# Staged blocks of a conditioned two-layer trunk: the written order is pinned on four engines, and the opening and the first quarter are rewritten

## The chip, the cores and the metric

The kernel runs on one core of a Trainium2 chip. The metric is the device time of one execution in microseconds; lower is better. A core has TensorE (PE, matrix products; PEld is its weight load), VectorE (DVE), ScalarE (ACT), GpSimd (POOL) and SyncE (SP, which here only issues transfers), each with its own instruction queue that is worked off in order, and 16 DMA engines that the queues share.

## The reference

Input x has 256 tokens of 2048 floats, c is one conditioning vector of 2048. There are two layers. In each, `mod = silu(c) @ ada_w[l] + ada_b[l]` gives six vectors of 2048: shift, scale and gate of the mixer, and shift, scale and gate of the feed-forward part (`ada_w[l]` is 2048 x 12288, 100 MB in float32). Then

```
h = rmsnorm(x) * norm_mix_g * (1 + scale) + shift
x = x + gate * mixer(h)          # layer 0: conv module | gated spatial unit; layer 1: pooling
h = rmsnorm(x) * norm_ffn_g * (1 + scale2) + shift2
x = x + gate2 * ((silu(h @ w1) * (h @ w3)) @ w2)
```

and at the end one more rmsnorm. The mixer of layer 0 multiplies h with `ab_w_in` (2048 x 4096); the feed-forward part with `w1` and `w3` (2048 x 5632). All weights are float32 and come from HBM once.

## The kernel before, in words

**Products.** Every weight is brought in as a `raw` tile of 256 rows by 512 columns (512 KB; `load`, L182, issued by SP into a pool of `RAW` = 12 buffers). `split` (L163) makes of it `hi` (a cast on ACT, L167) and `lo` (the remainder, on DVE, L168), four buffers each. A raw buffer is free again when lo is done. A *unit* (L198) is 512 rows by 512 columns, two raw tiles or halves; for each half and each of the two token halves b (128 tokens) there are four matmuls with hi (L216 with the activations' hi, L217 with their lo) and two with lo (L222): 24 matmuls a unit.

**Conditioning.** The scale and shift columns of a quarter (512 of 2048 features) are sums over four steps of two `ada_w` tiles each. `mod_cols` (L368) is a generator: a step loads two tiles and either multiplies them on PE (`ps_ada`, L381) or accumulates on DVE (`accq`, L388), and `put_cols` (L403) turns the sum into columns, by small matmuls into `ps_col`, with `sc`, `gs` or `sh` written by DVE. Scale goes over PE; shift over PE in quarter 0 and over DVE in the others.

**Entries.** For layer 0's mixer and its feed-forward part, `Entry` (L1024) holds the activations. `start` takes the reciprocal root of the mean square (DVE, POOL, L466 to L470); `prep` multiplies a quarter of x by it (`xr`, L477), transposes it on PE (L480) and copies it (`xT`, L518). Once the columns of a quarter are there, `scaled` (L492) applies scale and shift (ACT and DVE), and splits the result into `ah` (ACT) and `al` (DVE).

**Staged blocks.** `started` (L539) begins a projection before the columns of later quarters are known. For each quarter of the input features it scales, and then does three units, which accumulate over the quarters in three pairs of PSUM banks (two pairs `mm`, one pair `mt`). Between the halves of the units it advances the generators of the next quarter's columns (`between`, six slots a quarter). In layer 0's mixer, where nothing is known at the start, 48 MB have to come in for the block; there `params` (L627) runs after quarter 0: it transposes the spatial weights and the convolution's taps, and spreads two norm vectors over the partitions (`to_bcast`, L423), through a single PSUM buffer `ms`. In the feed-forward part of layer 0 the scale columns, and the shift columns up to quarter 1, come from background steps (`tick`, L280) that run with the units of the mixer.

**Order.** The program's text is not the order of the instructions. A scheduler orders them when the program is built, by priority (earlier text first) among those that it takes to be ready by its own estimate of times; each engine's stream is then fixed. A transfer waits in its queue until its buffer is free, and behind the transfers issued before it. The small tables are issued from ACT's queue at the start (L102, L121, L622 to L625), the two halves of x from SP ahead of the first ada tiles.

Of the kernel before, what the change touches and what calls it, by code (L numbers as in the profile page):

```python
# [8 lines left out]
F32 = mybir.dt.float32  # L9
F32R = mybir.dt.float32r  # L10
AF = mybir.ActivationFunctionType
ALU = mybir.AluOpType
PSUM = bass.MemoryType.PSUM

P = 128
# [21 lines left out]
class Trunk:  # L37
# [32 lines left out]
    def consts(self):  # L70
        nc, c = self.nc, self.cpool
        i = self.i
        cs = self.wk.tile([KT, P], F32, name="cs", tag="t", bufs=3)
        nc.sync.dma_start(out=cs, in_=i["c"].rearrange("a (k p) -> (a k) p", p=P))
# [12 lines left out]
        nc.gpsimd.memset(self.pick, 0.0)  # L87
        for j in range(4):
            nc.gpsimd.memset(self.pick[32 * j : 32 * j + 1, :], 1.0)

        ps = self.msp.tile([P, 512], F32, name="ps_c", tag="ms")
# [3 lines left out]
        stage = self.wk.tile([P, P], F32, name="stage", tag="t", bufs=3)  # L95
        nc.vector.memset(stage, 0.0)
# [10 lines left out]
        put("ffn_g", i["norm_ffn_g"].rearrange("l (k p) -> (l k) p", p=P), 2 * KT)  # L107
        put("conv_b", i["a_conv_b"].rearrange("l (k p) -> (l k) p", p=P), HT)
        put("a_g", i["a_norm_g"].rearrange("l (k p) -> (l k) p", p=P), HT)
        put("a_b", i["a_norm_b"].rearrange("l (k p) -> (l k) p", p=P), HT)  # L110
        put("b_bias", i["b_bias"].rearrange("l h t -> (l h) t"), HT)
        ps = self.msp.tile([P, 512], F32, name="ps_c", tag="ms")
        nc.tensor.transpose(ps[:, :P], stage, self.ident)
        cols = c.tile([P, P], F32, name="cols")
        nc.vector.tensor_copy(cols, ps[:, :P])
        self.col = lambda name, k: cols[:, rows[name] + k : rows[name] + k + 1]
        self.cols = lambda name, k, n: cols[:, rows[name] + k : rows[name] + k + n]
        self.adab = c.tile([P, 2, 6 * KT], F32, name="adab")
        for l in range(2):
            st = self.wk.tile([P, P], F32, name="st_b", tag="t", bufs=3)  # L120
            nc.scalar.dma_start(out=st[: 6 * KT, :], in_=i["ada_b"][l].rearrange("(k p) -> k p", p=P))  # L121
            ps = self.msp.tile([P, 512], F32, name="ps_b", tag="ms")
            nc.tensor.transpose(ps[:, : 6 * KT], st[: 6 * KT, :], self.ident[: 6 * KT, : 6 * KT])
            nc.vector.tensor_copy(self.adab[:, l, :], ps[:, : 6 * KT])

# [241 lines left out]

    def mod_cols(self, l, v, q, on_pe, dst, gname=None):  # L368

# [6 lines left out]
        for u in range(4):  # L376
            raws = [self.load(self.i["ada_w"][l], 512 * u + 256 * h, v * D + 512 * q) for h in range(2)]
            for j in range(4):
# [8 lines left out]
                else:  # L387
                    nc.vector.scalar_tensor_tensor(  # L388
                        acc, raws[j // 2][:, j % 2, :], self.cond[:, k : k + 1], acc, op0=ALU.mult, op1=ALU.add
                    )  # L390
            if u < 3:
                yield
# [4 lines left out]
        else:  # L397
            parts = [(acc, self.ones[:, :1])]
        yield
        self.put_cols(parts, 4, l, v, 4 * q, dst, gname)  # L400
# [35 lines left out]
    def norm_cols(self, e, l, sc, sh, gname):  # L436

        e.parts = [
            self.add(self.mod_cols(l, sc, q, True, e.gs, gname), self.mod_cols(l, sh, q, q == 0, e.sh))
            for q in range(4)  # L440
        ]
# [96 lines left out]

    def started(self, e, w_cols, rate, then=None):  # L539

        self.rate = 0.0
        ps = [self.banks(), self.banks()]
        ps.append([self.tpp.tile([P, 512], F32, name=f"mt{b}", tag="tp") for b in range(NB)])
        for g in e.parts[0]:
            self.close(g)
        for q in range(4):
# [56 lines left out]
    def mixer_ab(self, e, nxt):  # L605
        nc, i = self.nc, self.i
        with ExitStack() as s:
# [13 lines left out]
            nc.gpsimd.memset(nrm, 0.0)  # L621
            nc.scalar.dma_start(out=ws, in_=i["b_w_s"][0].rearrange("h t s -> t h s"))  # L622
            nc.scalar.dma_start(out=cwr[:CW, :], in_=i["a_conv_w"][0])
            for n, name in enumerate(("b_norm_g", "b_norm_b")):
                nc.scalar.dma_start(out=nrm[0:64:32, n, :], in_=i[name][0].rearrange("(j n) -> j n", n=512))  # L625

# [18 lines left out]

            for b in range(NB):
                e.start(b)
                for q in range(4):
                    e.prep(b, q)
            held = self.started(e, [(w_in, 0), (w_in, DH), (w_in, 512)], RATES[0], params)  # L650
            act = e.act
# [225 lines left out]
    def ffn(self, p, l, e, nxt, gen_g2, rest):  # L877
# [6 lines left out]
        if e.parts:  # L884
            for q in range(1, 4):
                e.prep(0, q)
            for q in range(4):
                e.prep(1, q)
            ps = self.started(e, [(w1, 0), (w3, 0), (w1, 512)], RATES[1])
            held = {(1, 0): ps[0], (3, 0): ps[1], (1, 1): ps[2]}  # L890
# [76 lines left out]
    def run(self):  # L967
        nc, i = self.nc, self.i
        self.ss = [None] * NB
        self.consts()  # L970
        self.x = []
        for b in range(NB):
            xb = self.xpool.tile([P, D], F32, name=f"x{b}")
            nc.sync.dma_start(out=xb, in_=i["x"][0, b * P : (b + 1) * P, :])
            self.x.append(xb)
            for q in range(4):
                self.sumsq(b, q)

# [9 lines left out]
        self.norm_cols(mix0, 0, SC1, SH1, "mix_g")  # L988
        self.finish(mix0.parts[0][:1])
        self.g1 = self.gate()  # L990
# [86 lines left out]
```

## Time and profile before

| | |
|---|---|
| median of 3 runs | 2014.65 us (2011.18 to 2015.0) |
| profiled execution | 2018.89 us, its span 2017.2 us |
| PE busy, chain of waits on PE | 97%, 95% |
| DVE, ACT, POOL busy | 70%, 42%, 2% |
| moved | 540.39 MB, 268 GB/s over the span |
| granted TensorE clock, mean | 0.982 |

The span is from the first to the last instruction of the profiled execution. A busy PE is one with a matmul in it, which doesn't mean that matmuls follow each other at full speed, so rates are read from the starts of matmuls. The granted clock is 1.0 at full speed and 0.5 after stretches with little work. A row of the timeline has start, duration, engine, line, operation, tiles and count, and in brackets the idle time before it and what ended it.

### The profile page before, as it was taken

To read this page: it belongs to the slowest core of one execution; us is meant where nothing else is said; L and a number is where in the kernel's file an instruction comes from. 1 tells how busy PE (TensorE), PEld (TensorE's weight loads), DVE (VectorE), ACT (ScalarE), POOL (GpSimd) and SP (SyncE) were. 2 spreads that over 40 slices of the span, in tenths; PEclk is the share of its full clock that TensorE was granted. 3 is DMA by queue.
4 is the path that set the end of the run, shared out by engine and by line. 5 is a ranking of instruction groups with operands and counts; after the bars stand their busy time and mean duration, and the time that the engine had idled before them with its cause. 6 is when DMAs were issued, how large, how long until landed. Compare 5 with 4: busy or idle time off the path is not lost.

```text
span 2017.2 us, 24298 instructions
## 1 busy us (share of the span) xinstructions
PE 1957.5 (97%) x8896; PEld 1542.4 (76%) x8896; DVE 1420.8 (70%) x1709; ACT 840.2 (42%) x1023; POOL 34.2 (2%) x91
## 2 busy tenths in 40 slices
PE   5989999998999999999999999999999999999998
PEld 2567677777887888887878887788788888888886
DVE  2667999788778888777887788867555444554455
ACT  3234343454444334443344347544433444334443
POOL 0000000000000000000120000000000000000000
PEclk9889999989999999999999999999999999999999
DMA  9998988879888899888988887889656666566651
GB/s 329 351 369 266 339 277 284 270 252 343 294 277 327 316 341 331 300 295 316 343 308 292 289 286 264 324 276 326 198 187 191 189 189 191 183 189 190 193 184 48
DMA packets 250344, 540.39 MB, mean 268 GB/s; under 512 B 16521, under 2 KB 17849, under 8 KB 249840
## 3 DMA queue, kind: packets, MB, share of 16 engines
q1 hardware_dynamic: 248472, 536.99, 78.2%
q10 hardware_dynamic: 1752, 1.86, 0.3%
q8 instruction: 69, 1.13, 0.2%
q14 instruction: 51, 0.42, 0.1%
HBM read 536.68 MB, written 2.10 MB: 267 GB/s over the span
## 4 chain that ended last, share of the span: by engine, by line
PE 95%; DVE 2%; DMA 2%; ACT 1%; issue 0%; POOL 0%; ACTq 0%; POOLq 0%; DVEq 0%
PE mm L216 28%; PE mm L217 27%; PE mm L222 27%; PE ps_ada L381 3%; PE ps_col L408 2%; PE mt L216 1%; PE mt L217 1%; PE tp L591 1%; PE mt L222 1%; DVE accq L388 1%; PE ps_ada L315 1%; PE tp L480 1%; DMA st_b<-in_ada_b_dram 1%; PE tp L838 1%; DMA raw<-in_pool_w_dram 0%
## 5 line engine op out<-in xcount | busy, mean ns | idle before, releaser
L167 ACT CAST hi<-raw 128x1024 fp32r<-128x1024 f32 x632 | 665.1, 1053 | 986.1 <-PE mm L217 898.2
L168 DVE TENSOR_TENSOR lo<-raw,hi 128x1024 fp32r<-128x1024 f32 x632 | 771.1, 1223 | 423.6 <-ACT hi L167 413.3
L216 PE MATMUL mm<-hi,ah 128*128 128x512 f32 x1568 | 619.5, 396 | 6.0 <-ACT hi L167 3.4
L217 PE MATMUL mm<-hi,al 128*128 128x512 f32 x1568 | 613.6, 392 | 0.0
L222 PE MATMUL mm<-lo,ah 128*128 128x512 f32 x1568 | 422.9, 390 | 0.0
L216 PEld LDWEIGHTS mm<-hi,ah 128*128 128x128 f32 x1568 | 296.0, 189 | 94.3 <-ACT hi L167 14.4
L217 PEld LDWEIGHTS mm<-hi,al 128*128 128x128 f32 x1568 | 296.1, 189 | 62.9 <-DVE accq L388 1.7
L222 PEld LDWEIGHTS mm<-lo,ah 128*128 128x128 f32 x1568 | 295.6, 189 | 61.7
L216 PE MATMUL mm<-hi,hh 128*128 128x512 f32 x704 | 279.9, 398 | 0.0
L217 PE MATMUL mm<-hi,hl 128*128 128x512 f32 x704 | 277.4, 394 | 0.0
L353 DVE SCALAR_TENSOR_TENSOR acc<-raw,cond,acc 128x1024 f32<-128x1024 f32 x180 | 230.6, 1281 | 5.3 <-DMA raw<-in_ada_w_dram 3.7
L222 PE MATMUL mm<-lo,hh 128*128 128x512 f32 x704 | 194.7, 395 | 0.0
L216 PEld LDWEIGHTS mm<-hi,hh 128*128 128x128 f32 x704 | 132.1, 188 | 34.7 <-ACT hi L167 1.7
L222 PEld LDWEIGHTS mm<-lo,hh 128*128 128x128 f32 x704 | 132.1, 188 | 32.1
L217 PEld LDWEIGHTS mm<-hi,hl 128*128 128x128 f32 x704 | 132.1, 188 | 30.8
L388 DVE SCALAR_TENSOR_TENSOR accq<-raw,cond,accq 128x512 f32<-128x512 f32 x135 | 101.1, 749 | 4.8 <-DMA raw<-in_ada_w_dram 2.1
L676 DVE SCALAR_TENSOR_TENSOR co<-aT,cw,co 128x256 f32<-128x256 f32 x240 | 99.5, 479 | 0.0
L216 PE MATMUL mm<-hi,mh 128*128 128x512 f32 x160 | 64.8, 406 | 1.6 <-ACT mh L489 1.6
L599 DVE TENSOR_TENSOR gy<-mm,gate 128x512 f32<-128x512 f32 x72 | 47.1, 686 | 24.3 <-PE mm L222 23.9
L217 PE MATMUL mm<-hi,ml 128*128 128x512 f32 x160 | 63.8, 401 | 0.3 <-DVE ml L490 0.3
L381 PE MATMUL ps_ada<-raw,cond 128*32 128x512 f32 x352 | 62.3, 629 | 0.0
L600 DVE TENSOR_TENSOR x<-x,gy 128x512 f32<-128x512 f32 x72 | 47.2, 688 | 0.1
(169 smaller groups left out, 990.6 us busy)
## 6 DMA issues: line engine op xcount, KB each, us to landing
raw<-in_ffn_w_dram SPq DMA_DIRECT2D x528, 512.0 KB, 4.8
raw<-in_ada_w_dram SPq DMA_DIRECT2D x384, 512.0 KB, 5.7
raw<-in_ab_w_in_dram SPq DMA_DIRECT2D x64, 512.0 KB, 6.5
raw<-in_ab_w_out_dram SPq DMA_DIRECT2D x32, 512.0 KB, 5.7
raw<-in_pool_w_dram SPq DMA_DIRECT2D x8, 512.0 KB
x<-in_x_dram SPq DMA_DIRECT2D x2, 1024.0 KB, 6.5
gate<-in_final_g_dram SPq DMA_DIRECT2D x1, 1024.0 KB
out_dram<-x SPq DMA_DIRECT2D x2, 512.0 KB
```

The source lines that it names most:

```text
L167: nc.scalar.copy(hi, raw)
L168: nc.vector.tensor_tensor(lo, raw, hi.bitcast(F32), op=ALU.subtract)
L216: nc.tensor.matmul(ps[b], act[b][0][:, kk, :], hi[:, k, :], start=first and kk == 0, stop=False)
L217: nc.tensor.matmul(ps[b], act[b][1][:, kk, :], hi[:, k, :], start=False, stop=False)
L222: self.nc.tensor.matmul(ps[b], act[b][0][:, kk, :], lo[:, k, :], start=False, stop=last and kk == 3)
L353: nc.vector.scalar_tensor_tensor(acc, raw, self.cond[:, k : k + 1], acc, op0=ALU.mult, op1=ALU.add)
L381: nc.tensor.matmul(acc[32 * j : 32 * j + 32, :], self.cond[:, k : k + 1].to_broadcast([P, 32]), raws[j // 2][:, j % 2, :], start=u == 0, s ...
L388: nc.vector.scalar_tensor_tensor(acc, raws[j // 2][:, j % 2, :], self.cond[:, k : k + 1], acc, op0=ALU.mult, op1=ALU.add)
L408: nc.tensor.matmul(ps[:, a : a + 1], src[:, P * a : P * a + P], one, start=u == 0, stop=u == len(parts) - 1,)
L599: nc.vector.tensor_tensor(t, ps, g[:, 512 * q : 512 * q + 512], op=ALU.mult)
L600: nc.vector.tensor_tensor(xs, xs, t, op=ALU.add)
L676: nc.vector.scalar_tensor_tensor(co[:, k, :], src, cw[:, k, j : j + 1], co[:, k, :], op0=ALU.mult, op1=ALU.add,)
```

## The change

`in_order` collects what is traced inside it and gives every instruction on PE, DVE, ACT and SP an edge to the one before it in the text on the same engine. The edges make no instruction wait at run time; they only forbid the scheduler another order. Both calls of `started` stand inside it, and in the mixer a new `opening` too, into which the loading of x, the small tables, the columns of quarter 0 and the preparation of both token halves have moved. The small tables are now issued by SP; the spatial weights, taps and norm vectors (`tables`) after quarter 0, and `params` follows quarter 1 rather than quarter 0.

In `started`, quarter 0 cuts the tiles of the first two units at once, and takes tokens 0 through both units before tokens 1; tokens 1 are scaled only then. In the feed-forward part the seven transposes after the first become hooks ahead of the half units. The other units are written out, with a slot for the generators behind each half; the staged columns (quarters 1 to 3 of the mixer) have one yield more after their last load and none before `put_cols`, so that the copy of the sum and `put_cols` stand together in the fifth slot.

```diff
+    @contextmanager
+    def in_order(self):
+        traced = self.nc.cur_bb.bb.instructions
+        n = len(traced)
+        yield
+        before = {}
+        for ins in traced[n:]:
+            if ins.engine in ORDERED:
+                if ins.engine in before:
+                    self.tc.add_manual_dep(ins, before[ins.engine].name, AFTER, reason="in_order")
+                before[ins.engine] = ins
...
+    def opening(self, e):
+        nc, c, i = self.nc, self.cpool, self.i
+        sc, sh = e.parts[0]
...
+        def tokens(b):
+            nc.sync.dma_start(out=self.x[b], in_=i["x"][0, b * P : (b + 1) * P, :])
+            for q in range(4):
+                self.sumsq(b, q)
+
+        def entry(b):
+            e.start(b)
+            for q in range(4):
+                e.prep(b, q)
...
-            nc.scalar.dma_start(out=stage[r : r + n, :], in_=ap)
+            nc.sync.dma_start(out=stage[r : r + n, :], in_=ap)
...
+        next(sc)
+        next(sc)
+        tokens(0)
+        next(sc)
         put("mix_g", i["norm_mix_g"].rearrange("l (k p) -> (l k) p", p=P), 2 * KT)
+        tokens(1)
+        entry(0)
+        next(sc)
         put("ffn_g", i["norm_ffn_g"].rearrange("l (k p) -> (l k) p", p=P), 2 * KT)
...
+        next(sh)
         put("conv_b", ...)
...
+        next(sh)
...
+            nc.tensor.transpose(ps[:, : 6 * KT], st[l][: 6 * KT, :], self.ident[: 6 * KT, : 6 * KT])
+            nc.vector.tensor_copy(self.adab[:, l, :], ps[:, : 6 * KT])
+        entry(1)
         ps = self.msp.tile([P, 512], F32, name="ps_c", tag="ms")
         nc.tensor.transpose(ps[:, :P], stage, self.ident)
...
+        self.close(sc)
+        next(sh)
+        next(sh)
+        self.close(sh)
...
         for q in range(4):
-            e.act[q] = [self.scaled(e.act[q][b], q, b, e.gs, e.sh) for b in range(NB)]
             nxt = e.parts[q + 1] if q < 3 else ()
+            if q == 0:
+                cuts = [cut(w, 0, col0) for w, col0 in w_cols[:2]]
+                for b in range(NB):
+                    e.act[0][b] = self.scaled(e.act[0][b], 0, b, e.gs, e.sh)
+                    for n in range(4):
+                        u, h = divmod(n, 2)
+                        for f in hooks.get((b, n), ()):
+                            f()
+                        self.products(*cuts[u][h], h, e.act[0], b, ps[u], True)
+                        self.products_lo(*cuts[u][h], h, e.act[0], b, ps[u], False)
+                        if h == 1:
+                            self.between(nxt, 2 * b + u)
...
+            else:
+                e.act[q] = [self.scaled(e.act[q][b], q, b, e.gs, e.sh) for b in range(NB)]
             for u, (w, col0) in enumerate(w_cols):
-                self.unit(
-                    w, 512 * q, col0, e.act[q], ps[u], q == 0, q == 3, lambda: self.between(nxt, 2 * u)
-                )
-                self.between(nxt, 2 * u + 1)
-            if q == 0 and then is not None:
-                then()
+                if q == 0 and u < 2:
+                    continue
+                for h, (hi, lo) in enumerate(cut(w, q, col0)):
+                    for b in range(NB):
+                        self.products(hi, lo, h, e.act[q], b, ps[u], q == 0)
+                    for b in range(NB):
+                        self.products_lo(hi, lo, h, e.act[q], b, ps[u], q == 3)
+                    self.between(nxt, 2 * u + h)
+                self.after_unit()
+            if q in then:
+                then[q]()
...
-            held = self.started(e, [(w_in, 0), (w_in, DH), (w_in, 512)], RATES[0], params)
+            with self.in_order():
+                self.opening(e)
+                held = self.started(
+                    e, [(w_in, 0), (w_in, DH), (w_in, 512)], RATES[0], {0: tables, 1: params}
+                )
...
+            late = [(1, 0), (0, 1), (1, 1), (0, 2), (1, 2), (0, 3), (1, 3)]
+            slots = [(0, 1), (0, 2), (0, 3), (1, 0), (1, 1), (1, 2), (1, 3)]
+            hooks = {at: [lambda c=c: e.prep(*c)] for at, c in zip(slots, late)}
+            with self.in_order():
+                ps = self.started(e, [(w1, 0), (w3, 0), (w1, 512)], RATES[1], hooks=hooks)
```

More of the change, by code (lines that the diff above doesn't have):

```diff
@@ L1 @@
-from contextlib import ExitStack
+from contextlib import ExitStack, contextmanager
 import concourse.bass as bass
@@ L13 @@
 PSUM = bass.MemoryType.PSUM
+ENG = mybir.EngineType
+ORDERED = (ENG.PE, ENG.DVE, ENG.Activation, ENG.SP)
+AFTER = mybir.DependencyInfo(mybir.DependencyClass.NoSync, mybir.DependencyReason.DATA)
 P = 128
@@ L101, in put @@
             nonlocal r
-            nc.scalar.dma_start(out=stage[r : r + n, :], in_=ap)
+            nc.sync.dma_start(out=stage[r : r + n, :], in_=ap)
             rows[name] = r
             r += n
+        next(sc)
+        next(sc)
+        tokens(0)
+        next(sc)
         put("mix_g", i["norm_mix_g"].rearrange("l (k p) -> (l k) p", p=P), 2 * KT)
+        tokens(1)
+        entry(0)
+        next(sc)
         put("ffn_g", i["norm_ffn_g"].rearrange("l (k p) -> (l k) p", p=P), 2 * KT)
+        st = [self.wk.tile([P, P], F32, name=f"st_b{l}", tag="t", bufs=3) for l in range(2)]
+        for l in range(2):
+            nc.sync.dma_start(out=st[l][: 6 * KT, :], in_=i["ada_b"][l].rearrange("(k p) -> k p", p=P))
+        next(sh)
         put("conv_b", i["a_conv_b"].rearrange("l (k p) -> (l k) p", p=P), HT)
@@ L111, in consts @@
         put("b_bias", i["b_bias"].rearrange("l h t -> (l h) t"), HT)
+        next(sh)
+        self.adab = c.tile([P, 2, 6 * KT], F32, name="adab")
+        for l in range(2):
+            ps = self.msp.tile([P, 512], F32, name="ps_b", tag="ms")
+            nc.tensor.transpose(ps[:, : 6 * KT], st[l][: 6 * KT, :], self.ident[: 6 * KT, : 6 * KT])
+            nc.vector.tensor_copy(self.adab[:, l, :], ps[:, : 6 * KT])
+        entry(1)
         ps = self.msp.tile([P, 512], F32, name="ps_c", tag="ms")
@@ L117, in consts @@
         self.cols = lambda name, k, n: cols[:, rows[name] + k : rows[name] + k + n]
[L118 to L124, printed above, removed]
+        self.close(sc)
+        next(sh)
+        next(sh)
+        self.close(sh)
     def bands(self, tiles):
@@ L366, in mod_full, with mod_cols @@
             yield
-    def mod_cols(self, l, v, q, on_pe, dst, gname=None):
+    def mod_cols(self, l, v, q, on_pe, dst, gname=None, staged=False):
         nc = self.nc
@@ L390, in mod_cols @@
                     )
-            if u < 3:
+            if u < 3 or staged:
                 yield
@@ L398, in mod_cols @@
             parts = [(acc, self.ones[:, :1])]
-        yield
+        if not staged:
+            yield
         self.put_cols(parts, 4, l, v, 4 * q, dst, gname)
@@ L438, in norm_cols @@
         e.parts = [
-            self.add(self.mod_cols(l, sc, q, True, e.gs, gname), self.mod_cols(l, sh, q, q == 0, e.sh))
+            self.add(
+                self.mod_cols(l, sc, q, True, e.gs, gname, staged=q > 0),
+                self.mod_cols(l, sh, q, q == 0, e.sh, staged=q > 0),
+            )
             for q in range(4)
@@ L543, in started, with cut @@
         self.rate = 0.0
         ps = [self.banks(), self.banks()]
[L545 removed]
         for g in e.parts[0]:
             self.close(g)
+        def cut(w, q, col0):
+            raws = [self.load(w, 512 * q + 256 * h, col0) for h in range(2)]
+            return [self.split(raw) for raw in raws]
         for q in range(4):
[L549 removed]
             nxt = e.parts[q + 1] if q < 3 else ()
[L551 to L557 removed]
+            if q == 0:
[10 more added lines that the diff above has]
+                            self.between(nxt, 2 * b + u)
+                for _ in range(2):
+                    self.after_unit()
+                ps.append([self.tpp.tile([P, 512], F32, name=f"mt{b}", tag="tp") for b in range(NB)])
+            else:
+                e.act[q] = [self.scaled(e.act[q][b], q, b, e.gs, e.sh) for b in range(NB)]
+            for u, (w, col0) in enumerate(w_cols):
+                if q == 0 and u < 2:
[6 more added lines that the diff above has]
+                    self.between(nxt, 2 * u + h)
+                self.after_unit()
+            if q in then:
+                then[q]()
@@ L621, in mixer_ab, with tables @@
             nc.gpsimd.memset(nrm, 0.0)
[L622 to L625, printed above, removed]
+            def tables():
+                nc.sync.dma_start(out=ws, in_=i["b_w_s"][0].rearrange("h t s -> t h s"))
+                nc.sync.dma_start(out=cwr[:CW, :], in_=i["a_conv_w"][0])
+                for n, name in enumerate(("b_norm_g", "b_norm_b")):
+                    nc.sync.dma_start(out=nrm[0:64:32, n, :], in_=i[name][0].rearrange("(j n) -> j n", n=512))
             def params():
@@ L644, in params @@
                 self.to_bcast(nrm[:, 1, :], bb, 2)
[L646 to L649, printed above, removed]
-            held = self.started(e, [(w_in, 0), (w_in, DH), (w_in, 512)], RATES[0], params)
+            with self.in_order():
+                self.opening(e)
+                held = self.started(
+                    e, [(w_in, 0), (w_in, DH), (w_in, 512)], RATES[0], {0: tables, 1: params}
+                )
             act = e.act
@@ L970, in run @@
         self.consts()
[L971 to L977, printed above, removed]
+        self.x = [self.xpool.tile([P, D], F32, name=f"x{b}") for b in range(NB)]
         def cols(name):
```

17 lines of the change are left out of this document (6 added, 11 removed).

## The prediction

> **What bounds the kernel now.** I read the page's totals, slices and chain of waits first, then a table of stretches, then the timeline of the two places that the change rewrites.
>
> ```profile
> span 2017.2 us, 24298 instructions
> PE 1957.5 (97%) x8896; PEld 1542.4 (76%) x8896; DVE 1420.8 (70%) x1709; ACT 840.2 (42%) x1023; POOL 34.2 (2%) x91
> GB/s 329 351 369 266 339 277 284 270 252 343 294 277 327 316 341 331 300 295 316 343 308 292 289 286 264 324 276 326 198 187 191 189 189 191 183 189 190 193 184 48
> PE 95%; DVE 2%; DMA 2%; ACT 1%; issue 0%; POOL 0%; ACTq 0%; POOLq 0%; DVEq 0%
> ```
>
> TensorE carries 95% of the chain, so a microsecond by which a staged block ends earlier or later is a microsecond at the end. The first three slices (some 150 us) move the most bytes. The next rows say why (columns: stretch, length, busy time of PE, PEld, DVE, ACT, POOL with counts, granted clock, DMA share, GB/s).
>
> ```profile
> 2.00:4.00 2.00, 0.26 (x1) 0.18 (x1) 0.00 (x0) 0.81 (x2) 1.02 (x2) 1.00 0.74 197
> 18.00:21.00 3.00, 0.13 (x1) 0.16 (x1) 0.00 (x0) 0.00 (x0) 0.00 (x0) 1.00 0.18 66
> 30.00:84.00 54.00, 44.21 (x209) 26.79 (x208) 28.80 (x47) 18.18 (x29) 0.00 (x0) 0.84 1.05 386
> 72.00:76.00 4.00, 3.65 (x14) 3.21 (x14) 3.02 (x7) 2.86 (x6) 0.00 (x0) 0.50 1.05 388
> ```
>
> From 30 to 84 us DMA is full at 386 GB/s and TensorE isn't: the first staged block is bound by the load stream. A load of 524 KB costs the stream 1.36 us. After a wait the clock is 0.50 (72 to 76), so a matmul then costs twice its time.
>
> ```profile
> 8.09 21.34 SPq L185 DMA_DIRECT2D raw<-in_ada_w_dram  x16
> 45.89 0.80 PE L216 MATMUL mm<-hi,ah 128*128 128x512 f32 x1 [3.39 <-ACT hi L167]
> 82.48 0.50 PE L216 MATMUL mm<-hi,ah 128*128 128x512 f32 x1
> 117.53 0.39 PE L216 MATMUL mm<-hi,ah 128*128 128x512 f32 x1
> 147.66 0.39 PE L216 MATMUL mm<-hi,ah 128*128 128x512 f32 x1
> 158.54 0.39 PE L216 MATMUL mt<-hi,ah 128*128 128x512 f32 x1
> 163.98 0.39 PE L216 MATMUL mm<-hi,ah 128*128 128x512 f32 x1
> ```
>
> These are the first products of quarters 0, 1, 2 and 3 of the first staged block, then the last unit and its end. A unit's 24 matmuls from 158.54 to 163.98 make 0.227 us each: 2.7 us for a half unit, 16.3 us for a quarter of three units. The block ends at 163.98; that is the number to beat.
>
> **The change, part by part.** Four engines now follow the text, so I walk the text with the durations of before. Loads are counted from 1 in SP's new order: 8 for the scale, 8 for the shift (x between them), 4 for the first two units, 16 for quarter 1's columns, 2 for the third unit, then 22 per quarter.
>
> *The opening.* The ada loads no longer wait till 8.09, so the stream flows from about 3 us (half of the stretch 2 to 4 was full) and load 12 lands near 26 us (8.5 MB at 386 GB/s, plus half a microsecond for small transfers queued between). From there the chain is one of small steps.
>
> ```profile
> 12.43 0.42 PE L123 MATMUL ps_b<-ident,st_b 96*128 96x96 f32 x1 [0.38 <-DVE cols L115]
> 12.88 0.26 DVE L124 COPY adab<-ps_b 128x96 f32<-128x96 f32 x1 [0.51 <-PE ps_b L123]
> 21.48 0.15 DVE L466 TENSOR_REDUCE s<-ss 128x1 f32<-128x4 f32 x1
> 22.49 1.28 DVE L477 TENSOR_SCALAR xr<-x,r 128x512 f32<-128x512 f32 x3 [0.68 <-POOL r L470]
> 36.16 4.55 PE L381 MATMUL ps_ada<-raw,cond 128*32 128x512 f32 x32
> 40.81 0.59 ACT L395 COPY rows<-ps_ada 128x512 f32<-128x512 f32 x1 [5.23 <-PE ps_ada L381]
> 41.45 1.05 PE L408 MATMUL ps_col<-pick,rows 128*128 128x1 f32 x8 [0.74 <-ACT rows L395]
> 435.02 3.20 PE L480 MATMUL tp<-ident,xr 128*128 128x128 f32 x12 [0.69 <-ACT xT L518]
> ```
>
> Shift step (a quarter of 4.55) to 27; two bias transposes with copies 1.7, to 28.7; the norm of tokens 1 (21.48 to 22.49) 1.0; xr and four transpose groups at 1.07 (3.20 for three) with the last copy 5, to 34.7; the table of columns 0.8; scale columns 1.1; two shift steps 2.2; rows 0.7; shift columns 1.1: 40.6. ScalarE casts the four waiting halves only behind the rows copy, and VectorE subtracts them before it scales the activations:
>
> ```profile
> L167 ACT CAST hi<-raw 128x1024 fp32r<-128x1024 f32 x632 | 665.1, 1053 | 986.1 <-PE mm L217 898.2
> L168 DVE TENSOR_TENSOR lo<-raw,hi 128x1024 fp32r<-128x1024 f32 x632 | 771.1, 1223 | 423.6 <-ACT hi L167 413.3
> L388 DVE SCALAR_TENSOR_TENSOR accq<-raw,cond,accq 128x512 f32<-128x512 f32 x135 | 101.1, 749 | 4.8 <-DMA raw<-in_ada_w_dram 2.1
> 73.14 0.88 ACT L500 ACTIVATE h<-xT,sh,gs 128x128 f32<-128x128 f32 x2 [4.01 <-DVE sh L414]
> 74.86 0.61 ACT L489 CAST ah<-h 128x512 fp32r<-128x512 f32 x1
> 76.78 0.69 DVE L490 TENSOR_TENSOR al<-h,ah 128x512 fp32r<-128x512 f32 x1
> ```
>
> Four lo at 1.22 from 40.6 end at 45.5, then 0.7 for h and 0.7 for ah: first product at 47.0 against 45.89. **The opening itself gains nothing**; it could lie 2 us to either side.
>
> *Tokens 0 ahead.* Unit 0 for tokens 0 at half clock 5.4 and its scale step 2, to 54.4; three more such pieces at 2.7 + 1.1, to 65.8. Nothing waits on tokens 1. Loads 33 and 34 need the buffers that the scale step at 54.4 frees, so the stream has a gap of some 3 us (0 if the clock is up at once) and load 38 lands near 64.3 (22.2 MB take 57.5, plus 3 and the gap). Third unit's first half 2.7, both column sums 2, scaling both token halves 2 x (0.88 + 0.61) = 3, next hi 1.05: quarter 1's first product at 74.7 against 82.48. **Here the change is 8 us ahead.**
>
> *Tables.* They leave ScalarE's queue at the start, where they shared the loss at 18 to 21, for SP's queue ahead of quarter 1's loads. The 512 KB of b_w_s cost 1.4. The 124 KB of a_conv_w cost 0.3 spread over 16 engines, or 124 KB / (386/16 GB/s) = 5.2 on one. In before its neighbour on that queue took long:
>
> ```profile
> 9.77 10.97 DMA st_b<-in_ada_b_dram
> ```
>
> 48 KB issued just behind it landed after 10.97 us, the end of it while DMA ran at 66 GB/s (18 to 21): a sixth of full, with something unfinished. That is nearest to one engine, so I take 4.9 beside the even share; both ends stay. So quarter 1's last load lands at 64.3 + 1.4 + 4.9 + 22 x 1.36 = 100.5.
>
> [...]
>
> *Params.* Before, its transposes and broadcasts lay between products (73 to 93). Now they stand in the text behind quarter 1, and quarter 2's scaling, splits, accumulations and products stand behind them on ACT, DVE and PE. One PSUM buffer makes them a chain:
>
> ```profile
> 83.28 0.60 PE L636 MATMUL tp<-ident,prm 128*128 128x128 f32 x4
> 83.92 0.69 DVE L637 COPY wcT<-tp 128x512 f32<-128x512 f32 x1 [1.04 <-PE tp L636]
> 84.73 0.43 PE L641 MATMUL tp<-ident,prm 31*128 31x31 f32 x4
> 85.20 0.29 DVE L642 COPY cw<-tp 128x124 f32<-128x124 f32 x1 [0.20 <-PE tp L641]
> 88.42 0.69 DVE L490 TENSOR_TENSOR rlo<-nrm,rhi 128x512 fp32r<-128x512 f32 x1 [0.71 <-PE ps_bc L432]
> 91.71 0.43 PE L432 MATMUL ps_bc<-rhi,identr 128*128 128x512 f32 x1
> 92.41 0.59 ACT L434 COPY bgb<-ps_bc 128x512 f32<-128x512 f32 x1 [0.82 <-PE ps_bc L433]
> ```
>
> Two rounds from 83.28 to 85.6 (2.33 each) are 4.7; four broadcasts at 1.4 (91.71 to 93.1) are 5.6; the two rlo that stand ahead of a pair add 1.4: 11.7. Counted from the last load (100.5): first half and column sums to +4.6, second half to +7.4, params to +19.1, scaling 3 and hi 1.05 to +23.2, that is 123.7; without params +8.9, 109.4. The twelve raw buffers cover 12 x 1.36 = 16.3 us of it, then DMA stands still for some 10. Quarter 2 can't catch up: its first piece runs at half clock (7.4), the next three take 3.8 each, the loads for its last column step can only be issued when the second step frees buffers, and VectorE has 4 lo and 16 accq (16.9) plus the last two lo before the turn. I get 28.9 to quarter 3's first product: 152.6 against 147.66. **The 8 us ahead have become 5 behind.** Plus 16.3: the block ends at 168.9, **+4.9**. If the chain cost nothing, quarter 3 would start at 100.5 + 8.9 + 29.9 = 139.3; that end of the bound is the rival below.
>
> *Second staged block.* Before:
>
> ```profile
> 430.75 0.66 PE L480 MATMUL tp<-ident,xr 128*128 128x128 f32 x4 [1.25 <-DVE xr L477]
> 442.72 0.79 PE L216 MATMUL mm<-hi,ah 128*128 128x512 f32 x1 [0.25 <-ACT ah L489]
> 503.32 2.27 PE mm L216 x4
> ```
>
> The first product can follow the first transpose group directly: 430.75 + 0.66 + copy 0.6 + 0.9 + 0.6 = 434 rather than 442.72. But seven groups (0.66) now lie between products, the first at half clock, so quarter 0 ends near 459.5; before it ended 19 us (16.3 and a cold start) after 442.72, near 462: 2.4 gained. Quarters 1 and 2 are bound by VectorE: 16 accq (12.0), 6 lo (7.3) and scaling (two al at 0.69, four h at some 0.3: 2.6) are 22, and in text order it also idles some 3 at a turn, when only the columns are awaited. 459.5 + 21.4 + 24.7 = 505.6 for the last quarter's first product, against 503.32 followed by 3 us lost to half clock. Together **-0.3**, bounded by -5 (all of the early start stays) and +4 (every accq delays a lo).
>
> Moved memsets and the two yields of the staged columns cost nothing: GpSimd is 2% busy, and the columns are summed behind a half unit of 2.7. If that cover were gone they would cost 2 per turn.
>
> **Sum:** +4.9 - 0.3 = about +5. The profiled execution took 2018.89 (span 2017.2) and would take 2024. The median of the runs, 2014.65, lies 4.2 below it: 2020.
>
> **Rivals.**
> - *It evens out, about 2015.* a_conv_w spreads (-4.9), or the stream has no gap at 55 us (-3). For it: each term is of the size of the sum. Against: the 10.97 us of its neighbour.
> - *Faster, about 2006.* The place is the turn from quarter 1 to quarter 2: if buffers and loads in flight hide the params chain, the stage stays bound by the stream and ends at 139.3 + 16.3 = 155.6, that is -8.4. For it: before, the same work cost little among products. Against: one PSUM buffer and the text order. It decides from the point where quarter 2's first product comes before 119 (123.7 - 4.9).
> - *Slower still, about 2026.* In the second block VectorE's fixed order (3.0 of accq ahead of each 1.22 of lo, against 2.7 of products) holds TensorE in each of eight slots: the +4 end, and the +5 stays, with some 2 more for half clock. For it: VectorE needs 22 per quarter and TensorE 16.3. Against: the slots lend each other time through four split buffers.
>
> **How the numbers follow.** Forecast (+2 to +9) 0.42, evens out 0.22, faster 0.27, slower still 0.09. The likeliest one's own range is 2016 to 2025. The range must reach the faster case's centre with some room, 2003, and the end of the slower one, 2029. What this kernel's runs can tell from no change is about 0.2%, 4 us: the forecast lies just above it. Slower takes most of the forecast and the slower case, 0.47; same 0.24; faster takes its rival and a little of the rest, 0.29.
>
> **What would show it.** Right: first product near 47, quarter 1's near 75, params rows in a stretch of some 12 us with hardly a product of the block in it and DMA well below 386 GB/s for about 10 us after it, quarter 2's first product near 124, end near 169; in the second block a first product near 434 and a last quarter that starts no earlier against the first block's end than before. Wrong: params rows with products between them, a first product before 42, or a first block that ends before 160.

## The result and the profile after

The changed kernel takes 2046.42 us (median of 4 runs, 2044.93 to 2048.26), the kernel before beside it on the same chip 2014.83 us: a ratio of 1.0158, interval 1.0139 to 1.0177. It is slower by 31.6 us, 27 more than forecast and 17 above the range. The profiled execution took 2047.44 us, 28.55 more than that of before.

From the page of the changed kernel (totals, slices, chain of waits):

```profile
span 2045.7 us, 24280 instructions
PE 1966.1 (96%) x8896; PEld 1545.2 (76%) x8896; DVE 1423.4 (70%) x1708; ACT 840.0 (41%) x1023; POOL 35.4 (2%) x92
GB/s 329 364 228 296 337 302 257 267 308 166 329 286 349 331 302 302 304 326 339 307 293 293 341 260 275 299 317 306 226 178 188 193 187 193 184 182 197 189 187 50
PE 87%; DVE 2%; DMA 1%; issue 1%; ACT 1%; POOL 0%; POOLq 0%; DVEq 0%; ACTq 0%
```

The busy times hardly move, but TensorE's share of the chain of waits falls from 95% to 87%, and two slices of the stream drop: the third (102 to 153 us) from 369 to 228 GB/s, the tenth (460 to 511) from 343 to 166. Those are the two staged blocks.

From the timeline of the changed kernel, the first products of quarters 0 to 3 and the first one behind the block, for the first block and then the second:

```profile
48.30 0.80 PE L249 MATMUL mm<-hi,ah 128*128 128x512 f32 x1 [6.03 <-ACT ah L526]
77.44 0.64 PE L249 MATMUL mm<-hi,ah 128*128 128x512 f32 x1 [2.58 <-ACT hi L200]
133.10 0.80 PE L249 MATMUL mm<-hi,ah 128*128 128x512 f32 x1 [4.99 <-ACT hi L200]
161.47 0.50 PE L249 MATMUL mm<-hi,ah 128*128 128x512 f32 x1 [1.82 <-ACT hi L200]
179.59 0.39 PE L249 MATMUL mm<-hi,ah 128*128 128x512 f32 x1
...
457.12 0.80 PE L249 MATMUL mm<-hi,ah 128*128 128x512 f32 x1 [7.47 <-ACT ah L526]
485.18 0.50 PE L249 MATMUL mm<-hi,ah 128*128 128x512 f32 x1 [0.77 <-ACT hi L200]
510.76 0.57 PE L249 MATMUL mm<-hi,ah 128*128 128x512 f32 x1
536.51 0.50 PE L249 MATMUL mm<-hi,ah 128*128 128x512 f32 x1 [0.28 <-ACT hi L200]
553.27 0.39 PE L249 MATMUL mm<-hi,ah 128*128 128x512 f32 x1
```

and the end of the second block in the kernel before:

```profile
522.72 0.39 PE L216 MATMUL mm<-hi,ah 128*128 128x512 f32 x1
```

The first block ends at 179.59 instead of 163.98: **+15.6**. From there to the end of the second block it is 373.7 us instead of 358.7: **+14.9**. Behind it 1494.2 are left instead of 1496.2: -2.0. Together that is the difference of the two profiled executions, 28.55.

**The turn to quarter 2.** The last load of quarter 1 is cast at 104.83; from then to 133.10 it is 28.3 us. Timeline of the changed kernel:

```profile
104.83 1.04 ACT L200 CAST hi<-raw 128x1024 fp32r<-128x1024 f32 x1 [0.30 <-DMA raw<-in_ab_w_in_dram]
112.45 0.63 PE L249 MATMUL mt<-hi,ah 128*128 128x512 f32 x1
112.88 0.63 PE L250 MATMUL mt<-hi,al 128*128 128x512 f32 x1
115.56 0.60 PE L715 MATMUL tp<-ident,prm 128*128 128x128 f32 x4
121.63 0.58 ACT L468 COPY bgb<-ps_bc 128x512 f32<-128x512 f32 x1 [14.76 <-PE ps_bc L467]
128.15 0.58 ACT L468 COPY bgb<-ps_bc 128x512 f32<-128x512 f32 x1 [1.31 <-PE ps_bc L467]
128.63 0.88 ACT L537 ACTIVATE h<-xT,sh,gs 128x128 f32<-128x128 f32 x2
```

Its table of stretches (columns as in the prediction):

```profile
115.00:120.00 5.00, 2.88 (x19) 2.02 (x17) 1.80 (x4) 0.00 (x0) 0.00 (x0) 0.84 0.22 81
120.00:125.00 5.00, 2.83 (x5) 1.37 (x5) 1.08 (x3) 1.69 (x3) 0.00 (x0) 0.50 0.00 2
125.00:130.00 5.00, 2.44 (x4) 0.79 (x3) 0.88 (x3) 2.41 (x5) 0.00 (x0) 0.50 0.00 0
130.00:135.00 5.00, 1.90 (x5) 1.53 (x6) 3.82 (x6) 4.45 (x8) 0.00 (x0) 0.50 0.00 0
```

The rows of params take 13.2 us (115.56 to 128.73). ScalarE waits 14.76 us for the first broadcast with everything of quarter 2 behind it, the transfers stand still for 15 us (the last column is 2, 0, 0), and the clock falls to 0.50.

**Quarter 0 of the second block.** Timeline of the changed kernel, then its table:

```profile
449.00 0.66 PE L517 MATMUL tp<-ident,xr 128*128 128x128 f32 x4 [1.25 <-DVE xr L514]
453.31 1.21 DVE L201 TENSOR_TENSOR lo<-raw,hi 128x1024 fp32r<-128x1024 f32 x1
455.21 26.19 SPq L218 DMA_DIRECT2D raw<-in_ada_w_dram  x4
456.02 0.34 DVE L539 TENSOR_SCALAR h<-xT,gs,sh 128x128 f32<-128x128 f32 x1
456.45 0.62 ACT L526 CAST ah<-h 128x512 fp32r<-128x512 f32 x1 [4.65 <-DVE h L539]
464.45 0.16 DVE L448 TENSOR_TENSOR sh<-ps_col,adab 128x4 f32<-128x4 f32 x1 [6.26 <-PE ps_col L442]
487.43 0.48 DVE L419 TENSOR_SCALAR accq<-raw,cond 128x512 f32<-128x512 f32 x1
```

```profile
457.00:465.00 8.00, 7.30 (x24) 5.69 (x24) 1.66 (x6) 0.65 (x2) 0.00 (x0) 0.60 0.43 162
465.00:481.00 16.00, 13.69 (x70) 10.91 (x71) 5.64 (x12) 7.58 (x13) 0.00 (x0) 1.00 0.01 2
```

For 16 us nothing is loaded (2 GB/s), while VectorE works 5.64 us of 16. SP's four loads from 455.21 take 26.19 us to issue: there is no free buffer. By the order of SP's loads two of the twelve buffers hold quarter 0's third unit and ten what quarter 1 and the next shift columns need. The first `accq` of those columns, which would free some, runs at 487.43, behind all of quarter 0 in the text. In the kernel before the same sum began at 450.91, in the middle of its quarter 0, where the scheduler had put it:

```profile
450.91 0.48 DVE L386 TENSOR_SCALAR accq<-raw,cond 128x512 f32<-128x512 f32 x1
460.00:465.00 5.00, 5.00 (x24) 4.14 (x23) 4.93 (x7) 2.11 (x2) 0.00 (x0) 1.00 1.05 381
```

### The profile page after: what moved, and what is told of

Read it like the earlier page. It is cut to its first block, busy times and chain, and to the rows that moved or that the text cites. A ratio compares the mean times of both kernels' runs of the same rounds, so it can differ in the third digit from the quotient of the medians.

```text
span 2045.7 us, 24280 instructions
## 1 busy us (share of the span) xinstructions
PE 1966.1 (96%) x8896; PEld 1545.2 (76%) x8896; DVE 1423.4 (70%) x1708; ACT 840.0 (41%) x1023; POOL 35.4 (2%) x92
## 3 DMA queue, kind: packets, MB, share of 16 engines
q10 hardware_dynamic: 288, 1.05, 0.1%
## 4 chain that ended last, share of the span: by engine, by line
PE 87%; DVE 2%; DMA 1%; issue 1%; ACT 1%; POOL 0%; POOLq 0%; DVEq 0%; ACTq 0%
PE mm L249 27%; PE mm L250 26%; PE mm L255 26%; PE ps_ada L414 1%; PE tp L668 1%; PE ps_col L442 1%; DMA raw<-in_ffn_w_dram 1%; PE ps_ada L348 1%; DVE accq L421 1%; DVE lo L201 1%; PE mt L255 1%; PE mt L249 1%; PE mt L250 1%; PE tp L917 1%; PE tp L517 0%
## 5 line engine op out<-in xcount | busy, mean ns | idle before, releaser
L421 DVE SCALAR_TENSOR_TENSOR accq<-raw,cond,accq 128x512 f32<-128x512 f32 x135 | 101.2, 750 | 13.8 <-DMA raw<-in_ada_w_dram 10.7
L255 PE MATMUL mm<-lo,mh 128*128 128x512 f32 x160 | 47.3, 405 | 0.0
```

The lines of the kernel that those rows point to most:

```text
L255: self.nc.tensor.matmul(ps[b], act[b][0][:, kk, :], lo[:, k, :], start=False, stop=last and kk == 3)
L421: nc.vector.scalar_tensor_tensor(acc, raws[j // 2][:, j % 2, :], self.cond[:, k : k + 1], acc, op0=ALU.mult, op1=ALU.add)
```

## The experiments

Each group was timed beside the kernel before on one chip; its median there was 2016.2 in the first group, 2016.64, 2017.22 and 2017.08 in the others. Differences are to that median ("over before"); the change itself is 31.6 over before.

**First group: the order or the text?** The written order was made a switch for each block, and in one kernel the instructions traced in `params` were left out of it.

```
-            if ins.engine in ORDERED:
+            if ins.engine in ORDERED and self.pins:
...
-        for ins in traced[n:]:
-            if ins.engine in ORDERED:
+        for k, ins in enumerate(traced[n:], n):
+            if ins.engine in ORDERED and not self.loose[0] <= k < self.loose[1]:
```

No order in either block:

> The changed kernel without any of the order edges: the new text, left to the scheduler. Theory A (the order edges cost the time, because ACT, DVE and SP can't go past what waits): most of the 31.6 us comes back, 2012 to 2024 us, and no stretch of ten us without DMA in either block. Rival B (the new text costs it: the opening, tokens 0 ahead, tables on SP): 2040 or more.

2020.63 us, ratio 1.0022 (1.0011 to 1.0033), 4.4 over before. Block 1 ends at 167.3, and block 2 takes 359.3 us from there.

Order in the mixer block alone, and in the feed-forward block alone:

> Order edges in the mixer's block alone. Theory A: the second block loses nothing against before, so some 12 us less than the changed kernel, about 2034 us; first block ends near 180 us as in the changed kernel. Rival B: about 2046 us, with the second block as slow as in the changed kernel.

> Order edges in the feed-forward block alone. Theory A: the first block ends near 164 us as before instead of 180, so about 2030 us; the second block still takes some 12 us more than before. Rival B: the first block ends near 180 us, about 2046 us.

2032.71 us, ratio 1.0083 (1.0061 to 1.0106): block 1 ends at 178.6, then 360.3 to the end of block 2. And 2030.14 us, ratio 1.0075 (1.0055 to 1.0096): 167.3, then 371.0. Against the run without an order, the order in one block alone costs 12.1 (mixer) and 9.5 us (feed-forward) by the medians. In both it costs 27.2, so 5.6 us more than the sum; what makes them isn't shown. The text without an order costs 4.4.

> Both blocks with their order edges, but the instructions of params left out of the edges, so that the scheduler may put them among the products of quarter 2. Theory A as the prediction put it (the params chain delays quarter 2 by some 14 us and the stream can't make it up): quarter 2 starts near 114 us instead of 133, the first block ends 12 to 16 us earlier, about 2032 us. Rival (the stream is what is late, by a_conv_w on one DMA engine and the late first quarter): the block ends at most 4 us earlier, about 2043 us.

2029.06 us, ratio 1.0070 (1.0050 to 1.0090). With params alone outside the order, block 1 ends at 165.6, 14 us earlier, and block 2 keeps its loss (372.1). That is no later than without any order (167.3): in block 1 the order costs nothing but at this one place.

**Second group: which engine, which load?** Four edits, each in a kernel of its own: VectorE left out of the order in the feed-forward block (`self.free`), a_conv_w in two loads, the order of SP alone, and no order with other places of tables and params (and a_conv_w in two loads there too).

```
-            if ins.engine in ORDERED:
+            if ins.engine in ORDERED and ins.engine not in self.free:
...
-                nc.sync.dma_start(out=cwr[:CW, :], in_=i["a_conv_w"][0])
+                for r0, r1 in ((0, 16), (16, CW)):
+                    nc.sync.dma_start(out=cwr[r0:r1, :], in_=i["a_conv_w"][0, r0:r1])
...
-ORDERED = (ENG.PE, ENG.DVE, ENG.Activation, ENG.SP)
+ORDERED = (ENG.SP,)
...
-RATES[0], {0: tables, 1: params}
+RATES[0], {0: params}, {(0, 0): [tables]}
```

> Everything as in the changed kernel, but in the feed-forward block VectorE's instructions are left out of the written order; the mixer block is pinned on all four engines as before. Theory A (in the second block the cost is VectorE's written order: the sums of the second column step stand behind quarter 0, so twelve buffers fill and the loads stop): the sums run during quarter 0 again, the stretch from 460 to 481 us moves well over 200 GB/s, the block lasts 84 us from its first product as with no written order there instead of 96, and the time is 2034 (2031 to 2038). Rival B (the cost lies in TensorE's or ScalarE's written order, the transpose groups between the products): the loads stop as before and the time stays above 2042.

2032.68 us, ratio 1.0086 (1.0068 to 1.0103); block 2 takes 357.4 us behind block 1. Theory A holds: in the stretch that it named, 460 to 481 us, the loads move 269 GB/s. Table of stretches and timeline of this run:

```profile
465.00:481.00 16.00, 15.77 (x76) 12.80 (x75) 15.67 (x21) 11.22 (x16) 0.00 (x0) 1.00 0.91 295
463.86 7.04 DVE L421 SCALAR_TENSOR_TENSOR accq<-raw,cond,accq 128x512 f32<-128x512 f32 x9
```

Nine `accq` in a row run in the middle of quarter 0; VectorE is busy 15.67 of 16 us instead of 5.64, and the stream moves 295 GB/s instead of 2. TensorE's transposes between the products, still pinned here, cost nothing that shows.

> The load of a_conv_w (31 rows) is issued as two, of 16 and of 15 rows; nothing else changes. Theory A (the 31 rows go over few DMA engines, so the stream runs at 106 to 319 GB/s from 72 to 78 us): this dip goes, the last load of quarter 1 lands 2 to 4 us earlier than 104.8, the first staged block ends as much earlier, and the time is 2043 (2041 to 2045). Rival B (the dip comes from full buffers, VectorE being late with the halves that free them): the dip stays and the time is 2046.

2038.45 us, ratio 1.0123 (1.0099 to 1.0146). The dip goes; first the changed kernel, then this one:

```profile
74.00:76.00 2.00, 0.86 (x4) 0.38 (x2) 1.26 (x4) 1.20 (x3) 0.00 (x0) 1.00 0.30 106
```

```profile
74.00:76.00 2.00, 2.00 (x14) 1.78 (x14) 0.76 (x3) 0.90 (x3) 0.00 (x0) 1.00 1.01 366
101.41 1.05 ACT L200 CAST hi<-raw 128x1024 fp32r<-128x1024 f32 x1 [0.32 <-DMA raw<-in_ab_w_in_dram]
```

The last load of quarter 1 is cast at 101.41 instead of 104.83, 3.4 us earlier, although the first product of this run comes 4.0 later (52.29; last section). The block's end comes 3.5 earlier (176.1), but the same pinned block ends at 178.6 and 177.1 in two other runs (order in the mixer block alone; VectorE free in the feed-forward block), so how much of this is the load's isn't shown. The time fell by more than that, some 8 us, below the expected range; another 3.2 lie between the blocks, in a part that no order holds, and 1.5 in the second block. What moved there isn't settled.

> Both blocks keep the written order of the loads (SP) alone; TensorE, VectorE and ScalarE are left free. Theory A (what costs is that work which is ready has to stand behind work which isn't, on the three computing engines): as with no written order at all, 2021 (2017 to 2025). Rival B (the order of the loads itself delays what is needed first): 2030 or more, with the first staged block's end past 172 us.

2020.07 us, ratio 1.0020 (1.0010 to 1.0031): as with no order at all. The order of the loads alone costs nothing that shows.

> The new text without any written order; the tables are issued behind the first four halves' loads, a_conv_w in two pieces, and the transposes and broadcasts of params stand behind quarter 0 as in the kernel before. Theory A (without the written order the new opening is 4 us ahead at its first product, and what it loses by the end of the first block, 3 us, comes from the tables and params standing later): the first block ends at 163 or before, 2014 (2010 to 2018). Rival B (the loss comes from the order of tokens 0 ahead of tokens 1 and its backlog on TensorE): 2020, with the first block's end near 167.

2013.65 us, ratio 0.9990 (0.9980 to 1.0000), 3.0 below before. Block 1 ends at 159.3. The 4.4 us of the text without an order were the places of tables and params and the 31-row load together, not tokens 0 ahead of tokens 1, which stays here.

**Third group: does it add up, and is it the place or the order?**

> As the run with no written order and early tables, but the feed-forward block has the text of the kernel before (all transposes ahead, the quarters unit by unit). Theory A (without a written order the new text of the second block costs some 4 us by itself: there the block took 84.3 us from its first product to its end, before it took 80.0): what the first block gains, 8.6 us at the second block's first product, reaches the end, and the time is 2010 (2006 to 2013). Rival B (the gain is given back after the second block whatever its text, by transfers that were ahead anyway): 2013 to 2015.

2013.46 us, ratio 0.9988 (0.9978 to 0.9997): no gain from the old text of the second block. It takes 358.8 us behind the first with it and 359.1 with the new text. Theory A falls: that the span from the first product differs (80 to 84 us) only says that this product comes earlier.

> As the changed kernel with its written order, with two things left out of it: the instructions of params in the mixer block, and VectorE in the feed-forward block. Theory A (these two places are the whole cost of the written order, each by work that stands behind something that waits): each gave 17 and 14 us by itself, together 2016 (2013 to 2020). Rival B (the gains overlap, what one gives is lost at the other): 2025 or more.

2019.81 us, ratio 1.0023 (1.0011 to 1.0035), 2.6 over before. With the order kept everywhere but for params in the mixer block and VectorE in the feed-forward block, 29 of the 31.6 us are gone.

> As the run beside it with both places left out of the written order, and a_conv_w loaded in two pieces of 16 and 15 rows. Theory A (the 31 rows cost the stream 2 to 3 us where it bounds the block): 2 to 4 us below the run beside it. Rival B (once the stalls are gone the block is bound elsewhere, or the 8 us that this edit gave in the changed kernel were the clock's phase or another order of the free part): within 1 us of it.

2013.57 us, ratio 0.9990 (0.9979 to 1.0001): 6.2 below its neighbour, more than expected. The last load of quarter 1, first in the neighbour, then in this run:

```profile
106.00 1.05 ACT L200 CAST hi<-raw 128x1024 fp32r<-128x1024 f32 x1 [0.31 <-DMA raw<-in_ab_w_in_dram]
```

```profile
99.55 1.05 ACT L200 CAST hi<-raw 128x1024 fp32r<-128x1024 f32 x1 [0.31 <-DMA raw<-in_ab_w_in_dram]
```

It is cast 6.45 us earlier, but here the first products lie 3.6 apart the other way (52.06 and 48.42), ahead of the edited load. So both pairs mix the load with the opening, with opposite signs. With the 31 rows in one load the cast comes at 103.9 to 104.8 where the first product comes at 48 to 49 (three runs: the changed kernel, and those with the order in the mixer block alone and with VectorE free), and at 105.6 to 106.5 where it comes at 52 (three runs: params outside the order, params last, and the neighbour). In two pieces it comes at 99.55 and 101.41. At the same opening the load costs 4.2 to 5.3 us, and the later opening some 1.8.

> The changed kernel with all its written order, but params stands behind quarter 3 of the mixer block instead of behind quarter 1. Theory A (the chain costs what is queued behind it: at the turn it holds the scaling and the splits that free the buffers, at the end only work outside the written order follows): quarter 2's first product comes near 119, no stretch without transfers, the first block's products end near 166, and the time is 2032 (2028 to 2036). Rival B (the chain costs its 13 us wherever it stands, then with the convolution waiting for its results): 2042 or more.

```
-                    e, [(w_in, 0), (w_in, DH), (w_in, 512)], RATES[0], {0: tables, 1: params}
+                    e, [(w_in, 0), (w_in, DH), (w_in, 512)], RATES[0], {0: tables, 3: params}
```

2033.73 us, ratio 1.0090 (1.0072 to 1.0108). Timeline and table of stretches of this run:

```profile
116.74 0.50 PE L249 MATMUL mm<-hi,ah 128*128 128x512 f32 x1 [0.46 <-ACT hi L200]
115.00:120.00 5.00, 4.54 (x19) 2.79 (x22) 3.97 (x6) 2.52 (x3) 0.00 (x0) 0.84 0.49 155
120.00:125.00 5.00, 5.00 (x30) 2.65 (x23) 4.79 (x8) 2.11 (x2) 0.00 (x0) 1.00 0.98 346
```

Quarter 2 starts at 116.74, 16.4 us earlier than with params in front of it, and block 1 ends at 164.2, 15.4 earlier; 2.9 of that are lost again by the end of block 2. The same instructions under the same order cost little where nothing pinned stands behind them, as theory A says.

**Fourth group: the opening.** The loads of `ada_b` and their transposes were moved ahead of the transposes of tokens 0, in the changed kernel and in two of the better ones.

```
         next(sc)
         next(sc)
+        st = [self.wk.tile([P, P], F32, name=f"st_b{l}", tag="t", bufs=3) for l in range(2)]
+        for l in range(2):
+            nc.sync.dma_start(out=st[l][: 6 * KT, :], in_=i["ada_b"][l].rearrange("(k p) -> k p", p=P))
         tokens(0)
...
         tokens(1)
+        self.adab = c.tile([P, 2, 6 * KT], F32, name="adab")
+        for l in range(2):
+            ps = self.msp.tile([P, 512], F32, name="ps_b", tag="ms")
+            nc.tensor.transpose(ps[:, : 6 * KT], st[l][: 6 * KT, :], self.ident[: 6 * KT, : 6 * KT])
+            nc.vector.tensor_copy(self.adab[:, l, :], ps[:, : 6 * KT])
         entry(0)
...
```

> The changed kernel, with the two loads of ada_b issued behind the fourth load of the scale step and their transposes ahead of the transposes of tokens 0, so that they no longer wait for buffers that the scaled tokens hold; all the written order stays. Theory A (the wait of SP at 17.31 and 21.60 us leaves the stream standing for 4 us, and the first block is bound by the stream): no stretch under 100 GB/s between 16 and 24 us, the last load of quarter 1 lands 3 to 4 us earlier than 104.8, the first block ends as much earlier, time 2043 (2041 to 2045). Rival B (the opening is bound by its chain of small steps and the gap is made up for while buffers fill): the stream's gap goes but the last load of quarter 1 lands within 1 us of 104.8, time 2046.

2037.04 us, ratio 1.0100 (1.0082 to 1.0118), less than theory A's range. What the wait was, in the changed kernel:

```profile
17.31 0.33 SPq L135 DMA_DIRECT2D st_b<-in_ada_b_dram  x1
21.60 0.33 SPq L135 DMA_DIRECT2D st_b<-in_ada_b_dram  x1
20.00:22.00 2.00, 1.55 (x7) 1.55 (x8) 0.00 (x0) 1.28 (x3) 0.00 (x0) 0.50 0.00 0
```

and in this run:

```profile
20.00:24.00 4.00, 4.00 (x20) 3.12 (x24) 2.52 (x8) 2.76 (x6) 0.55 (x1) 0.50 1.05 373
41.80 0.79 PE L249 MATMUL mm<-hi,ah 128*128 128x512 f32 x1 [6.10 <-ACT ah L526]
100.22 1.04 ACT L200 CAST hi<-raw 128x1024 fp32r<-128x1024 f32 x1 [0.31 <-DMA raw<-in_ab_w_in_dram]
```

The stream has no gap, the first product comes 6.5 us earlier, the last load of quarter 1 4.6 earlier, and block 1 ends 4.7 earlier (174.85); the profiled execution is 4.8 us shorter. The other runs of this kernel are shorter still (2035.56 to 2037.81), and over before it is 11.6 less by the medians (20.0 against 31.6); what lies between 4.8 and 11.6 no profile shows.

> The same edit in the kernel whose written order leaves out params in the mixer block and VectorE in the feed-forward block, with a_conv_w in two pieces (2013.57 without this edit). Theory A: 3 to 4 us below that, 2010 (2007 to 2012), below the kernel before by more than its measurement is uncertain. Rival B: 2013.5.

**2007.75 us, ratio 0.9959 (0.9944 to 0.9974)**: faster than both kernels, and the only one here whose whole interval lies more than 0.2% below before. Its landmarks in the timeline, first product, end of block 1, end of block 2:

```profile
41.64 0.79 PE L249 MATMUL mm<-hi,ah 128*128 128x512 f32 x1 [7.13 <-ACT ah L526]
153.50 0.39 PE L249 MATMUL mm<-hi,ah 128*128 128x512 f32 x1
513.38 0.39 PE L249 MATMUL mm<-hi,ah 128*128 128x512 f32 x1
```

> The same edit in the kernel without any written order, with early tables (2013.65 without this edit). There the stream's dip is shorter (some 203 GB/s from 18 to 22 us in the run without a written order). Theory A: 1 to 2 us less, 2012 (2009 to 2013). Rival B: 2013.5.

2012.83 us, ratio 0.9980 (0.9971 to 0.9989), 0.8 less than without the edit, and 1.3 less over before: the times don't decide between the two theories. In the profiled runs the dip is gone (from 18 to 22 us 383 GB/s instead of 220), and yet block 1 ends no earlier (159.6, and 159.3 without the edit), which is rival B. That end is 6 us later than in the kernel with the loosened order. The two also differ in the places of tables and params, so that it is the order which is better is not shown.

## Why the prediction was right in its sign and wrong in its size

In the profiled executions the forecast was +4.6 (4.9 - 0.3) and the measurement 28.55. Of the 23.9 between them 15.2 lie in the second block and 10.7 in the first; 2.0 go the other way behind them.

**Opening: 47.0 forecast, 48.30 measured, by luck.** The step "load 12 lands near 26 us" was wrong. SP's order puts the two bias loads in front of the shift's ada loads, and their buffers are of the three that the scaled tokens (`xr`) share; so SP waits to 21.60 and the stream stands. The prediction walked the bias rows' transposes and not the buffer of their load. The shift step ended at 31.84 instead of 27, and the chain behind it took 16.5 us instead of 20, which nearly cancels it. In four of the eight profiled runs with this opening the first product comes at 52, outside the 2 us that the forecast allowed (last section). The 3 us gap that it had put at 55 us isn't there (387 GB/s from 54 to 64). Quarter 1 started at 77.44, not 74.7, and the last load was cast at 104.83, not 100.5: 4.3 late, and the run that mends the opening has it at 100.22.

**Tables: right.** The term of 4.9 for the 31 rows was the author's estimate, from the 386 GB/s over 16 engines and the 10.97 us of its neighbour. In the runs the load costs 4.2 to 5.3 at the same opening, and the cost goes with 16 and 15 rows. In the trace of before, 23 to 29 GB/s move from 19.5 to 21 us, at a DMA share of 0.06 to 0.08, about one engine of 16; whose bytes these are, and over how many engines the 31 rows went, isn't shown.

**Params: right mechanism, mis-sized.** The "params rows in a stretch of some 12 us" took 13.2, and "DMA well below 386 GB/s for about 10 us" became 15 with hardly a load. The turn was forecast at 23.2 and took 28.3: the third unit and the column sums 10.7 instead of 7.4, params 13.2 instead of 11.7, scaling and cast 4.4 instead of 4.05. The missing term is TensorE's clock: the prediction priced the turn's matmuls at 0.227 us, and the rows at 112.45 and 112.88 lie 0.43 apart (granted clock 0.66 from 105 to 110, 0.50 from 112 to 115). Quarter 2 took 28.4 (28.9 forecast). The last quarter took 18.1 instead of 16.3. So 168.9 + 4.3 + 5.1 - 0.5 + 1.8 = 179.6.

**Second block: the step that failed.** Forecast -0.3, bounded by -5 and +4; measured +14.9 from end to end of the blocks. "The first product can follow the first transpose group directly" took 8.1 us instead of 3.3, since two `lo` and the sums stand ahead of `h` on VectorE (453.31 to 456.02). Quarters 0, 1 and 2 took 28.1, 25.6 and 25.8 instead of 25.5, 21.4 and 24.7, and the first transposes came 2.6 later behind block 1 than in the kernel before; that makes up the miss. The upper bound priced VectorE's order as throughput, every sum delaying a `lo`. It was the other way round: sums and splits wait behind quarter 0, VectorE idles, twelve buffers fill and the stream stops for 16 us, twelve loads' worth at 1.36. The prediction counted the twelve buffers at the turn to quarter 2 and didn't count them here. Freeing VectorE alone brought the block to 357.4.

**The rivals.** "It evens out" had a condition come true, no gap at 55 us, but the stream lost as much earlier, and the 31 rows did cost it. "Faster" had its deciding point about right, a first product of quarter 2 before 119: the runs that take params away from the turn have it at 118.9 and 116.74, and there block 1 ends at 165.6 and 164.2, near the 163.98 of before; with 107.31 (the fastest run) it ends at 153.50. Its mechanism failed: twelve buffers didn't hide the chain, and the stream stood. The text order, which the prediction gave against it, is what decided. "Slower still" had the right block and engine, and a mechanism that the runs contradict: it needs a busy VectorE.

**Range.** One block's loss alone would have ended at the edge of it (2014.65 + 13.9 = 2028.6, or + 16.5 = 2031.2); two didn't fit. Its upper end took +4 for all that an order could do in the second block, and nothing in the trace bounded that.

## What to carry to other kernels

An order written over all engines turns each late result into a wait for everything behind it (here 14.76 us of ScalarE for one broadcast, and 26.19 us for four loads of SP), also on engines that don't need it. So for every instruction that waits in the text, list what is queued behind it that would *free buffers*, and hold the number of buffers times the price of a load against the wait; do it at every turn of the text, and for the small loads on SP's queue too. Here an order with two sets of instructions left out of it, the 31-row load in two pieces and two small loads moved was faster than both kernels (0.9959), though the full order costs 1.6%.

## What the runs showed of the hardware that was not expected

The opening's time depends on the clock granted to TensorE, which differs between runs of the same text. The changed kernel and the run with a_conv_w in two pieces have the same order up to the first product, and yet it comes at 48.30 and 52.29. The eight small matmuls behind the table of columns show why, first the changed kernel, then the other:

```profile
37.53 1.05 PE L442 MATMUL ps_col<-pick,rows 128*128 128x1 f32 x8 [0.38 <-DVE cols L151]
```

```profile
38.18 1.87 PE L442 MATMUL ps_col<-pick,rows 128*128 128x1 f32 x8 [0.38 <-DVE cols L151]
```

They run at full speed in one and near half in the other, with the same idle time ahead (granted clock from 36 to 38 us: 1.00 and 0.50). Eight profiled runs have this opening. In four these matmuls take 1.05 us and the first product comes at 48.30 to 49.11; in the other four they take 1.87 and it comes at 51.92 to 52.29. So 4 us are at stake; what sets the clock no run here shows. Little work alone doesn't: in the kernel before, TensorE is busy for 0.13 us of the 6 from 15 to 21, and the clock from 21 to 26 is 1.00, while 1.98 us of the 6 from 66 to 72 are followed by 0.50 (72 to 76). Nor was it shown that the clock is behind the spread of 2037.37 to 2045.48 among the runs of one kernel.

Two profiled runs that differ by one edit can therefore differ by the opening as well. That is why the cost of the 31-row load came out only from runs with the same first product.
